# Stores on GpSimd's queue, loads on SyncE's queue, the first norm's gain applied in PSUM evictions, and dilated attention with the two heads of a pair side by side

## The chip, the cores and the metric

The kernel runs on one core of one Trainium2 chip. The metric is device time in microseconds (us) of one execution of the whole program. Engines are named as in the profile: PE is TensorE's matmuls, PEld its weight loads, DVE is VectorE, ACT is ScalarE, POOL is GpSimd, SP is SyncE. SPq and POOLq rows are the DMA issues of these two queues.

## The reference, cut to what matters

Two layers work on one sequence of 1024 tokens of width 1024, all in float32.

```
first_block:   h = rmsnorm(x, norm_gain);  proj = h @ w_in
               o_a = attention over all 1024 keys (8 query heads, 2 key heads, rotary) * silu(g_a)
               o_b = neighbourhood attention on a 16 x 64 grid (8 heads of 64)          * silu(g_b)
               x = x + [o_a, o_b] @ w_out;  x = rmsnorm(x, final_norm_gain)
second_block:  h = rmsnorm(x, norm_w);     proj = h @ w_in_2
               y_dn  = gated delta rule, 4 heads of 128, chunks of 64
               y_att = dilated attention, 8 heads of 64, patterns (window, dilation) =
                       (128, 1), (512, 4), (2048, 16), joined by their log-sum-exp, * silu(gate)
               x = x + [y_dn, y_att] @ w_out_2
```

The first norm is `x * rsqrt(mean(x*x) + eps) * norm_gain`, and the gain is one factor for each of the 1024 channels. A query of a dilated pattern sees the keys of its residue class in its own block and the block before it.

## The kernel before, in words

Tokens lie in eight tiles of 128. A product in full precision is made of three float32r matmuls: each operand is split into a rounded high part (ACT copies, `hh` or `whi`) and the rest (DVE subtracts, `hl` or `wlo`).

The **opening** (lines 549 to 575) loads the eight tiles of x (512 KB each) and the gain `ng`, repeated over 128 partitions (another 512 KB). It takes the tiles two at a time: ACT squares each tile with a row sum (line 561), DVE finds the inverse root in eleven small steps (`rs_of`, lines 286 to 297), and the tile is multiplied by the gain (line 563) and the root (lines 570 to 574). `H1.put` then transposes a tile by PE in two PSUM banks of four 128 x 128 blocks, and evicts each bank with one ACT copy (`hh`, line 315) and one DVE subtraction (`hl`, line 316), both 128 x 512. The first weights are loaded in `fill1` (line 1061) and split by lines 354 and 355.

After that two streams share the engines. `main` runs the attentions and the delta rule; `fill` runs the projections and the output products. `share` (line 465) emits them in turn by the PE time they have spent, and the Tile scheduler orders each engine's instructions by priority and by its own simulated clock. The order on an engine or a queue is then fixed.

**Queues.** `ld` and `st` are both SyncE's queue (lines 185 and 187), and so are four stores that are written with `ld` (lines 592, 603, 1350, 1364). `gl` is GpSimd's queue and has only the operands of the neighbourhood attention (`k2`, `vv` and `qT`, lines 795, 796 and 824): 44 loads. A DMA whose data or buffer isn't ready holds everything behind it on its queue. Many results go through DRAM: stored by one stage and loaded by a later one (`qa_d`, `bq_d`, `o_d`, `xp_d`, `raw_d`, `ab_d`, `tb_d`, `n_d`, `yp_d`). Stores leave from small staging buffers; the `e5` pool has four of 256 KB, which weights and residual rows are loaded into as well (line 519).

**Dilated attention** (`jobs_c`, line 1544) runs for four pairs of heads j. A pair has 24 items of 128 queries: eight of the pattern with dilation 4 (strided by 4 in q and k; half of them have one key tile, half two), eight of the pattern with dilation 16 (strided by 8, one key tile), and eight of the dense pattern (the first has one key tile, the others two). An item (line 1556) makes for each head two score matmuls (`qq` and `ql` as weights, `k2` as the moving operand, 128 or 256 columns), a masked minimum on DVE (line 1568), an exponential on ACT (1570), transposes of P on PE, a copy to `PTc` on ACT (1581), and the value matmuls (line 1588): float32, which the trace records as two passes each, with 64 columns of `v` moving, for one head. DVE copies the result to N (1592). While a pair is in work, `prep_c` prepares the next. `fill` at that time is `first_part(2, ...)` (line 909), in half-tiles of 12 matmuls of 512 columns: each loads a residual row block into an `e5` buffer (line 915), adds the product (917 or 919) and stores it (920) to `yp_d`. Its second part waits until the pairs 0 to 2 are done.

Of the kernel before, what the change touches and what calls it, by code (L numbers as in the profile page):

```python
# [32 lines left out]
NT = 8  # L33
KC = 8
# [26 lines left out]
SC = ['s']  # L61
SD = ['s']
XPR = 5000
XS = 1
LASTC = {1: 6, 2: 7}
LEAD2 = 1000.0
LEAD3 = 1000.0
# [7 lines left out]
LB = 1000.0  # L75
KO = 1
CP = 'S'
CO = 'V'
CHP = 0
AHP = 0  # L80
BHP = 0
# [72 lines left out]
def hybrid_kernel(ctx: ExitStack, tc: tile.TileContext, A, out, dbg=None, upto=99):  # L154
    nc = tc.nc
    V, S = nc.vector, nc.scalar
# [26 lines left out]

    PE = _PE()
    ld = nc.sync.dma_start
    gl = nc.gpsimd.dma_start
    st = nc.sync.dma_start
    dbg = dbg or {}

    def dram(t, off, ap):  # L190
        return bass.AP(tensor=t.tensor, offset=t.offset + off, ap=ap)
# [4 lines left out]
    sm = ctx.enter_context(tc.tile_pool(name="sm", bufs=3))  # L196
# [33 lines left out]
    def tbank():  # L230
        half[0] ^= 256
        return po_[:, half[0]:half[0] + 256]
# [13 lines left out]
    def wbank():  # L246
        return bank("w")
# [7 lines left out]
    def f32(t):  # L255
        return t.bitcast(F32)
# [13 lines left out]
    ident = f32(identr)  # L270
# [271 lines left out]
    r_d = dp.tile([8, 1024], F32, name="r_d")  # L542


    w1 = A["w_in"][0]
    H = {}
    hr.open("h1")
    H1 = Tr(hr, KC)
    with tc.tile_pool(name="xp", bufs=2, reuse_waits="tile") as xp:
        ng = xp.tile([128, 1024], F32, name="ng", bufs=1)  # L550
        for b in range(0, NT, 2):
            ss = sm.tile([128, 2], F32, name="ssx")
            xg = []
            for i in (b, b + 1):
                xt = xp.tile([128, 1024], F32, name="xt", bufs=8)
                with tc.high_priority(XPR):
                    ld(xt, grid(x_in, i))
                    if i == 0:
                        ld(ng, dram(A["norm_gain"], 0, [[0, 128], [1, 1024]]))
                scr = xp.tile([128, 1024], F32, name="sqrow", bufs=1)  # L560
                S.activation(scr, xt, AF.Square, accum_out=ss[:, i - b:i - b + 1])
                if b:
                    V.tensor_tensor(xt, xt, ng, op=OP.mult)
                xg.append(xt)
            rs = rs_of(ss, 2, 1.0 / 1024)
            for i in (b, b + 1):
                xn = xg[i - b]
                r1 = rs[:, i - b:i - b + 1]
                if b and i % 2 and XS:
                    S.activation(xn, xn, AF.Copy, scale=r1)  # L570
                elif b:
                    V.tensor_scalar(xn, xn, r1, None, op0=OP.mult)
                else:
                    V.scalar_tensor_tensor(xn, xn, r1, ng, op0=OP.mult, op1=OP.mult)
                H1.put(xn, i)

    def make_bias():
        rb = wk.tile([33, 8], F32, name="rb")
        V.memset(rb, 1.0)
        tb8 = wk.tile([8, 32], F32, name="tb8")  # L580
        ld(tb8, A["rel_bias_2"])
        tb = tbank()
        PE.transpose(tb[0:32, 0:8], tb8, ident[0:8, 0:8])
        V.tensor_copy(rb[0:32], tb[0:32, 0:8])
        oh = wk.tile([33, 1024], F32, name="oh")
        ld(oh, A["oh"])
        rr = wk.tile([8, 1024], F32, name="rr")
        for c in range(2):
            tb = sbank()
            PE.matmul(tb[0:8, :], rb, oh[:, c * 512:(c + 1) * 512], start=True, stop=True)  # L590
            V.tensor_copy(rr[:, c * 512:(c + 1) * 512], tb[0:8, :])
        ld(r_d, rr)


    wk.open("rpp")
    if 1:
        make_bias()
        rp = wk.tile([8, 32, 48], F32, name="rp")
        V.memset(rp, 0.0)
        r0 = wk.tile([8, 15, 31], F32, name="rp0")  # L600
        ld(r0, A["na_rpb"][0])
        V.tensor_scalar(rp[:, 8:23, 8:39], r0[:, ::-1, ::-1], 8.0, None, op0=OP.mult)
        ld(rp_d, rp)
    wk.close()

    def finish_pair(o2, den2, dst):
# [182 lines left out]
    def prep_b(j, B):  # L789

        yield from wait("B%d" % j)
        k2 = wm.tile([128, 2, 1024], F32R, name="k2", bufs=2)
        vv = wm.tile([128, NT, 2, 128], F32, name="vv", bufs=2).rearrange("p t h d -> p (t h d)")[:, 0:1024].rearrange("p (t c) -> p t c", t=NT)
        for a in range(2):
            gl(k2[64 * a:64 * a + 64], dram(bq_d[j], (2 + a) * 128 * 1024, [[1024, 64], [64 * 1024, 2], [1, 1024]]))
        gl(vv, bv_d[j].rearrange("(t p) c -> p t c", p=128))
        if j == 0:
            wk.close()
            wk.open("pb")
        if j == 0:  # L800
            masks.append(wk.tile([128, 3, 3, 16, 8], F32, name="masks"))
            ld(masks[0].rearrange("p v g r c -> p (v g r c)"), A["c1"][:, 1152:2304])
        tab = wk.tile([128, 2, 3, 384], F32, name="tab", bufs=2)
        B[j] = k2, vv, tab
        for h in range(2):

            tr = wk.tile([128, 16, 64], F32, name="tr")
            t3 = tr.rearrange("p r c -> p (r c)")[:, 0:768]
            ld(t3, dram(rp_d, (2 * j + h) * 32 * 48, [[48, 16], [1, 8], [1, 768]]))
            t3 = t3.rearrange("p (r c) -> p r c", c=48)[:, ::-1, ::-1]  # L810
            for v in range(3):
                V.tensor_tensor(tab[:, h, v].rearrange("p (g r c) -> p g r c", g=3, c=8),
                    t3[:, :, 24 - 8 * v:48 - 8 * v].rearrange("p r (g c) -> p g r c", c=8), masks[0][:, v], op=OP.add)
        yield 0.5

    def attn_b(j, B, live, then=None):
        k2, vv, tab = B.pop(j)
        qTs = {}

        def prep(b):  # L820

            qTs[b] = wk.tile([128, 4, 256], F32R, name="qT", bufs=QB)
            for a in range(2):
                gl(qTs[b][64 * a:64 * a + 64], dram(bq_d[j], b * 256, [[1024, 64], [64 * 1024, 4], [1, 256]]))

        def item(i, h, qT, two):

# [230 lines left out]
        yield from mark("op1")  # L1058

    def fill1():  # L1060
        ws, _ = load_w(w1, [(512, 0, 1, 256), (0, 0, 1, 256)])
# [91 lines left out]
    def delta_main():  # L1153
# [20 lines left out]
        def main2():  # L1174
# [164 lines left out]
            def chain(u):  # L1339
# [5 lines left out]
                for k in range(2):  # L1345
                    am = tc4()
                    V.tensor_tensor(am, Hs[k]["An"], bm[:, None, :].to_broadcast([128, 4, 128]), op=OP.mult)
                    ac = wk.tile([128, 4, 16], F32, name="ac", bufs=2)
                    V.tensor_reduce(ac, am.rearrange("p t (b c) -> p t c b", c=16), op=OP.add, axis=AX.X)
                    ld(dram(ab_d[u], k * 8192, [[16, 128], [2048, 4], [1, 16]]), ac)  # L1350
# [7 lines left out]
                for r in range(1, 16):  # L1358
# [5 lines left out]
                ld(tb_d[u], Tn.rearrange("p r c -> p (r c)"))  # L1364


                def join(mask, Tn_, Tt, H):
# [176 lines left out]
    def jobs_c(j):  # L1544
# [11 lines left out]
        def item(q, k, vs, T, N, then=None):  # L1556
# [2 lines left out]
            nkt = len(vs)  # L1559
            nk = 128 * nkt  # L1560
            s = sbank()
            sh = [s[:, h * nk:(h + 1) * nk] for h in range(2)]
            for h in range(2):
                PE.matmul(sh[h], qq[:, h, q], k2[:, h, k], start=True, stop=False)
                PE.matmul(sh[h], ql[:, h, q], k2[:, h, k], start=False, stop=True)
            P = wk.tile([128, 2, 256], F32, name="Pc", bufs=CB)
            for h in range(2):
                V.tensor_tensor_reduce(out=P[:, h, :nk], in0=sh[h], in1=T[:, h, T.shape[2] - nk:], op0=OP.add, op1=OP.min,  # L1568
# [16 lines left out]
            o = pbank()  # L1585
            for h in range(2):
                for t, v in enumerate(vs):
                    PE.matmul(o[:, h * 64:h * 64 + 64], PT[:, h * nkt + t], v[:, h], start=t == 0, stop=t == nkt - 1)
            if CO[alt[0] % len(CO)] == "S":
                S.activation(N[:, 0:128], o[:, 0:128], AF.Copy)  # L1590
            else:
                V.tensor_copy(N[:, 0:128], o[:, 0:128])  # L1592
            if then:
                then()
            yield 0.43 * nkt
# [127 lines left out]
```

## Time and profile before

| | us |
|---|---|
| median of 3 runs | 1762.08 |
| lowest and highest | 1745.34, 1762.79 |
| the profiled execution, in all | 1749.34 |
| its span on the core | 1747.6 |
| PE busy (share of the span) | 1560.6 (89%) |
| DVE busy | 1121.8 (64%) |
| ACT busy | 785.3 (45%) |
| POOL busy | 28.5 (2%) |
| mean granted TensorE clock, as a share of full | 0.937 |
| moved by SyncE's queue / by GpSimd's queue | 188.34 MB / 14.68 MB |

The busy share of PE is an average over stages, and its matmul records overlap, so 89% does not mean that 11% is idle everywhere. The slices of the page and the windows of the trace show which stages have idle time. A granted clock of 1.0 is 2.4 GHz, and 0.5 is 1.2 GHz.

### The profile page before, as it was taken

How to read it: one execution, taken by the hardware profiler on the slowest of the kernel's cores; microseconds unless marked ns; L12 is line 12 of the kernel's file. 1: busy time of each engine (PE TensorE's matmuls, PEld its weight loads, DVE VectorE, ACT ScalarE, POOL GpSimd, SP SyncE). 2: the span in 40 equal slices, each digit the busy share in tenths (PEclk: the TensorE clock that was granted, in tenths of full speed). 3: DMA queues.
4: the chain of work that ended last, by engine and by line, in shares of the span. 5: the costliest groups of instructions: out<-in, count | busy, mean ns of one | idle time of the engine just before them, and what ended most of it. 6: DMA issues, size and time to landing. Idle time of an engine off the chain costs nothing. (4 is left out here: it accounts for less than half of the span.)

```text
span 1747.6 us, 27569 instructions
## 1 busy us (share of the span) xinstructions
PE 1560.6 (89%) x9362; PEld 1377.5 (79%) x9362; DVE 1121.8 (64%) x3469; ACT 785.3 (45%) x2189; POOL 28.5 (2%) x48
## 2 busy tenths in 40 slices
PE   1988999999999789996799999998999489899997
PEld 1877788989898677885677788887889478788985
DVE  5679866666573554558545768676677575767646
ACT  5235445445452432544344443534524352765631
POOL 0000000000001101100000000000000000000000
PEclk8999999999999889997899999999999879876999
DMA  7011121422226998875344323314322555433476
GB/s 173 17 61 51 56 80 63 102 79 56 83 71 162 199 256 194 223 208 145 76 113 98 96 74 85 97 51 108 91 61 71 166 174 162 136 93 87 119 229 219
DMA packets 212825, 204.79 MB, mean 117 GB/s; under 512 B 27363, under 2 KB 164763, under 8 KB 212684
## 3 DMA queue, kind: packets, MB, share of 16 engines
q1 hardware_dynamic: 202252, 188.34, 38.4%
q0 software_dynamic: 10432, 14.68, 4.9%
q8 instruction: 74, 1.21, 0.3%
q14 instruction: 67, 0.55, 0.1%
HBM read 131.83 MB, written 71.13 MB: 116 GB/s over the span
## 5 line engine op out<-in xcount | busy, mean ns | idle before, releaser
L172 PE MATMUL pw<-whi,hh 128*128 128x512 f32 (+2 forms) x1032 | 359.1, 350 | 10.5 <-DVE e L524 5.4
L172 PE MATMUL pw<-wlo,hh 128*128 128x512 f32 (+2 forms) x1032 | 357.1, 346 | 0.3 <-DVE wlo L355 0.3
L172 PE MATMUL pw<-whi,hl 128*128 128x512 f32 (+2 forms) x1032 | 356.3, 345 | 0.0
L172 PEld LDWEIGHTS pw<-whi,hh 128*128 128x128 f32 x1032 | 196.9, 192 | 31.9 <-DVE e L524 6.0
L172 PEld LDWEIGHTS pw<-wlo,hh 128*128 128x128 f32 x1032 | 197.8, 192 | 19.6 <-DVE wlo L355 0.5
L172 PEld LDWEIGHTS pw<-whi,hl 128*128 128x128 f32 x1032 | 197.4, 191 | 19.9
L355 DVE TENSOR_TENSOR wlo<-e,whi 128x512 fp32r<-128x512 f32 (+3 forms) x168 | 103.6, 624 | 73.3 <-ACT whi L354 72.3
L354 ACT ACTIVATE whi<-e 128x512 fp32r<-128x512 f32 (+3 forms) x168 | 95.3, 581 | 96.9 <-DMA e<-in_w_in_dram 71.0
L172 PE MATMUL pw<-hh,whi 128*128 128x512 f32 x320 | 129.8, 405 | 7.6 <-ACT whi L354 7.5
L172 PE MATMUL pw<-hl,whi 128*128 128x512 f32 x320 | 127.2, 398 | 0.0
L172 PE MATMUL pw<-hh,wlo 128*128 128x512 f32 x320 | 123.3, 399 | 0.0
L172 PEld LDWEIGHTS po<-vc,PTc 128*128 128x128 f32 x560 | 87.9, 228 | 12.1 <-DVE N L1592 5.4
L172 PE MATMUL po<-vc,PTc 128*128 128x64 f32 x560 | 90.2, 304 | 7.3 <-DVE N L1592 4.2
L172 PE MATMUL s<-k,qT 128*128 128x512 f32 (+1 forms) x282 | 90.1, 407 | 2.7 <-ACT PT L845 1.3
L1568 DVE CUSTOM_DVE_ANT_0 Pc<-s,tab 128x128 f32<-128x128 f32 (+1 forms) x192 | 59.6, 348 | 39.5 <-PE s L172 26.4
L172 PE MATMUL po<-PT,vv 128*128 128x256 f32 x512 | 75.9, 288 | 3.9 <-DVE PT L745 3.2
L172 PEld LDWEIGHTS pw<-hh,whi 128*128 128x128 f32 x320 | 61.1, 191 | 23.2 <-ACT whi L354 11.2
L172 PEld LDWEIGHTS po<-PT,vv 128*128 128x128 f32 x512 | 68.7, 193 | 8.7 <-DVE PT L745 5.1
L745 DVE TENSOR_TENSOR PT<-s,PT 128x512 fp32r<-128x512 f32 x77 | 52.3, 685 | 32.2 <-ACT PT L744 23.1
L736 ACT ACTIVATE P<-s,nm 128x512 f32<-128x512 f32 x77 | 52.6, 686 | 44.7 <-DVE nm L733 41.9
L840 ACT ACTIVATE Pb<-Pb,m 128x384 f32<-128x384 f32 x64 | 39.1, 612 | 73.3 <-DVE m L838 70.6
L172 PEld LDWEIGHTS pw<-hl,whi 128*128 128x128 f32 x320 | 61.2, 191 | 11.4
(398 smaller groups left out, 3364.8 us busy)
## 6 DMA issues: line engine op xcount, KB each, us to landing
e<-in_w_in_dram SPq DMA_DIRECT2D x72, 256.0 KB, 3.7
bq_d<-e SPq DMA_DIRECT2D x32, 256.0 KB, 2.2
qT<-bq_d POOLq DMA_DIRECT2D x32, 256.0 KB, 7.4
e<-in_w_out_dram SPq DMA_DIRECT2D x32, 256.0 KB, 5.9
xp_d<-mx SPq DMA_DIRECT2D x32, 256.0 KB, 3.9
yp_d<-e SPq DMA_DIRECT2D x32, 256.0 KB, 3.3
e<-in_w_in_dram SPq DMA_DIRECT2D x32, 192.0 KB, 3.4
raw_d<-e SPq DMA_DIRECT2D x24, 256.0 KB, 2.0
```

What stands on the lines that cost most here:

```text
L172: self.last = f(*a, **k).ins
L354: S.activation(hi[:, :n], raw[:, :n], AF.Copy)
L355: V.tensor_tensor(lo[:, :n], raw[:, :n], f32(hi[:, :n]), op=OP.subtract)
L736: S.activation(P[:, hf * 512:(hf + 1) * 512], ss[hf], AF.Exp, bias=nm[:, 2:3], accum_out=den[:, h, hf:hf + 1])
L745: V.tensor_tensor(dl, by4(tb), f32(dh), op=OP.subtract)
L840: S.activation(P, P, AF.Exp, bias=nm, scale=-1.0, accum_out=den[:, h:h + 1])
L1568: V.tensor_tensor_reduce(out=P[:, h, :nk], in0=sh[h], in1=T[:, h, T.shape[2] - nk:], op0=OP.add, op1=OP.min, scale=-1.0, scalar=3e38, accu ...
```

## The change

1. `st` becomes GpSimd's queue, and `gl` is dropped, so that every load is on SyncE's queue. The four stores that were written with `ld` are now written with `st`. The loads of `k2` and `qT` are declared as float32 on both sides.
2. The opening loads x in two groups of four tiles and the first weights between them in program order. The gain is loaded as 8 x 128 and transposed once by PE, so that it stands as one column of 128 factors for each channel block. The tiles are only scaled by the root. The transposes of two tiles (for the last four, of four tiles) share a bank, and the evictions apply the gain: one ACT copy with a scale and one DVE operation for each channel block, 128 x 256 for the first four tiles and 128 x 512 for the last four.
3. In dilated attention an item with one key tile multiplies each head's queries with the keys of both heads (256 columns moving), and uses the half that belongs to it. The value matmul of each head has the values of both heads moving (128 columns), and the copy to N picks the two blocks that are wanted.

```diff
-    gl = nc.gpsimd.dma_start
-    st = nc.sync.dma_start
+    st = nc.gpsimd.dma_start
...
+        g8 = xp.tile([8, 128], F32, name="g8", bufs=1)
+        ld(g8, dram(A["norm_gain"], 0, [[128, 8], [1, 128]]))
...
+        def load_x(tiles):
+            for i in tiles:
                 xt = xp.tile([128, 1024], F32, name="xt", bufs=8)
                 with tc.high_priority(XPR):
                     ld(xt, grid(x_in, i))
...
+        def normed(b):
+            ss = sm.tile([128, 2], F32, name="ssx")
+            for i in (b, b + 1):
+                scr = xp.tile([128, 1024], F32, name="sqrow", bufs=2)
+                S.activation(scr, xts[i], AF.Square, accum_out=ss[:, i - b:i - b + 1])
             rs = rs_of(ss, 2, 1.0 / 1024)
+            V.tensor_scalar(xts[b], xts[b], rs[:, 0:1], None, op0=OP.mult)
+            if b < 4:
+                V.tensor_scalar(xts[b + 1], xts[b + 1], rs[:, 1:2], None, op0=OP.mult)
+            else:
+                S.activation(xts[b + 1], xts[b + 1], AF.Copy, scale=rs[:, 1:2])
+        def flip_x(tiles, gT):
+            n = len(tiles)
+            h, l = H1.half(tiles[0] // 4)
+            c = slice(tiles[0] % 4 * 128, (tiles[0] % 4 + n) * 128)
+            m = 4 // n
+            for k0 in range(0, KC, m):
+                tb = wbank()
+                for k in range(m):
+                    for j, i in enumerate(tiles):
+                        PE.transpose(tb[:, (k * n + j) * 128:(k * n + j + 1) * 128], xts[i][:, (k0 + k) * 128:(k0 + k + 1) * 128], ident)
+                for k in range(m):
+                    t, g = tb[:, k * n * 128:(k + 1) * n * 128], gT[:, k0 + k:k0 + k + 1]
+                    S.activation(h[:, k0 + k, c], t, AF.Copy, scale=g)
+                    V.scalar_tensor_tensor(l[:, k0 + k, c], t, g, f32(h[:, k0 + k, c]), op0=OP.mult, op1=OP.subtract)
+        load_x(range(4))
...
+        for b in (0, 2):
+            normed(b)
+            flip_x((b, b + 1), gT)
+            if b == 0:
+                ws0 += load_w(w1, [(512, 0, 1, 256), (0, 0, 1, 256)])[0]
+                load_x(range(4, 8))
+        for b in (4, 6):
+            normed(b)
+        flip_x((4, 5, 6, 7), gT)
...
-            gl(k2[64 * a:64 * a + 64], dram(bq_d[j], ...))
-        gl(vv, bv_d[j].rearrange("(t p) c -> p t c", p=128))
+            ld(f32(k2[64 * a:64 * a + 64]), dram(bq_d[j].bitcast(F32), ...))
+        ld(vv, bv_d[j].rearrange("(t p) c -> p t c", p=128))
...
-            sh = [s[:, h * nk:(h + 1) * nk] for h in range(2)]
+            sh = [s[:, h * 256:(h + 1) * 256] for h in range(2)]
             for h in range(2):
-                PE.matmul(sh[h], qq[:, h, q], k2[:, h, k], start=True, stop=False)
-                PE.matmul(sh[h], ql[:, h, q], k2[:, h, k], start=False, stop=True)
+                kk = k2[:, h, k] if nkt == 2 else k2[:, :, k]
+                PE.matmul(sh[h], qq[:, h, q], kk, start=True, stop=False)
+                PE.matmul(sh[h], ql[:, h, q], kk, start=False, stop=True)
+            if nkt == 1:
+                sh = [s[:, h * 384:h * 384 + 128] for h in range(2)]
...
-                    PE.matmul(o[:, h * 64:h * 64 + 64], PT[:, h * nkt + t], v[:, h], start=t == 0, stop=t == nkt - 1)
+                    PE.matmul(o[:, h * 128:h * 128 + 128], PT[:, h * nkt + t], v.rearrange("p h d -> p (h d)"),
+                              start=t == 0, stop=t == nkt - 1)
...
-                V.tensor_copy(N[:, 0:128], o[:, 0:128])
+            V.tensor_copy(N[:, 0:128].rearrange("p (h d) -> p h d", h=2), o.rearrange("p (a d) -> p a d", d=64)[:, 0::3])
```

## Rows read from the trace of the kernel before

**Rows 1.** The page, part 2: the granted clock in 40 slices, in tenths of full speed.

```profile
PEclk8999999999999889997899999999999879876999
```

**Rows 2.** Windows: stretch, length, then busy PE, PEld, DVE, ACT, POOL, clock, DMA, GB/s.

```profile
1000.00:1200.00 200.00, 196.59 (x1144) 171.43 (x1142) 141.10 (x397) 87.11 (x247) 0.00 (x0) 0.99 0.34 83
1380.00:1404.00 24.00, 0.14 (x1) 0.17 (x2) 9.89 (x43) 6.96 (x22) 0.00 (x0) 0.54 0.65 192
1490.00:1660.00 170.00, 155.71 (x915) 146.25 (x916) 117.95 (x509) 111.61 (x390) 0.00 (x0) 0.81 0.38 109
1539.00:1559.00 20.00, 19.47 (x94) 19.13 (x94) 9.97 (x52) 10.20 (x42) 0.00 (x0) 0.50 0.37 107
```

**Rows 3.** Timeline of the opening: start, length, instruction, [idle before and its end].

```profile
3.39 0.51 SPq L559 DMA_DIRECT2D ng<-in_norm_gain_dram  x1
...
13.65 1.06 ACT L561 ACTIVATE sqrow<-xt 128x1024 f32<-128x1024 f32 x1 [3.23 <-DMA xt<-in_x_dram]
...
15.88 1.06 ACT L561 ACTIVATE sqrow<-xt 128x1024 f32<-128x1024 f32 x1 [1.08 <-DMA xt<-in_x_dram]
...
24.87 2.48 DVE L574 SCALAR_TENSOR_TENSOR xt<-xt,rq_y,ng 128x1024 f32<-128x1024 f32 x2
...
26.30 1.08 PE L172 MATMUL s<-ident,xt 128*128 128x128 f32 x4 [26.30 <-DVE xt L574]
...
49.28 0.39 PE L172 MATMUL pw<-whi,hh 128*128 128x256 f32 x1 [0.53 <-DVE rb L579]
```

**Rows 4.** Groups of DVE instructions in the first 50 us: total, mean ns, idle before.

```profile
L563 DVE TENSOR_TENSOR xt<-xt,ng 128x1024 f32<-128x1024 f32 x6 | 7.3, 1224 | 3.1 <-ACT sqrow L561 3.0
...
L316 DVE TENSOR_TENSOR hl<-s,hh 128x512 fp32r<-128x512 f32 x8 | 5.4, 682 | 1.3 <-ACT hh L315 1.3
...
L572 DVE TENSOR_SCALAR xt<-xt,rq_y 128x1024 f32<-128x1024 f32 x3 | 2.2, 748 | 0.0
L289 DVE TENSOR_TENSOR rq_a<-rq_y 128x2 f32<-128x2 f32 x12 | 1.7, 154 | 0.1
```

**Rows 5.** Timeline where the delta rule ends: SyncE's issues around a store, and PE's next matmul.

```profile
1373.51 0.42 SPq L889 DMA_DIRECT2D e<-g_d  x1
...
1384.22 2.29 SPq L1452 DMA_DIRECT2D o_d<-orr  x2
...
1386.56 0.98 SPq L1487 DMA_DIRECT2D trc<-r_d  x2
...
1403.86 1.08 PE L172 MATMUL pw<-ident,e 128*128 128x128 f32 x4 [23.89 <-DVE rq_ac L290]
```

**Rows 6.** Timeline of PE: float32 matmuls of the delta rule, dilated scores, value matmuls.

```profile
1060.33 1.06 PE L172 MATMUL s<-Tt,da 128*128 128x128 f32 x8
...
1377.32 1.29 PE L172 MATMUL s<-da,da 128*128 128x256 f32 x4
1378.80 1.16 PE L172 MATMUL s<-da,da 128*128 128x128 f32 x4
...
1464.94 1.19 PE L172 MATMUL s<-da,da 128*128 128x128 f32 x4
...
1704.18 1.00 PE L172 MATMUL po<-vc,PTc 128*128 128x64 f32 x8
```

**Rows 7.** DMA issues (KB each, median us to landing), then landing times of GpSimd's qT loads.

```profile
yp_d<-e SPq DMA_DIRECT2D x32, 256.0 KB, 3.3
...
e<-yp_d SPq DMA_DIRECT2D x16, 256.0 KB, 4.1
...
DMA to landing us min/median/max: 3.7/7.4/11.9
```

**Rows 8.** Waits of the queues: total us, times, longest.

```profile
SPq L915 <- DMA yp_d<-e: 51.4, 23, 5.0
...
POOL qT L824 <- PE s L172: 121.2, 10, 24.1
```

**Rows 9.** The chain of waits: start, length, piece, with the count of its instructions.

```profile
1669.36 4.12 PE pw L172 x18
```

More of the change, by code (lines that the diff above doesn't have):

```diff
@@ L63 @@
 XPR = 5000
-XS = 1
 LASTC = {1: 6, 2: 7}
@@ L77 @@
 CP = 'S'
-CO = 'V'
 CHP = 0
@@ L548, in hybrid_kernel @@
     H1 = Tr(hr, KC)
+    ws0 = []
     with tc.tile_pool(name="xp", bufs=2, reuse_waits="tile") as xp:
[L550 to L554, printed above, removed]
+        g8 = xp.tile([8, 128], F32, name="g8", bufs=1)
+        ld(g8, dram(A["norm_gain"], 0, [[128, 8], [1, 128]]))
+        xts = []
+        def load_x(tiles):
+            for i in tiles:
                 xt = xp.tile([128, 1024], F32, name="xt", bufs=8)
@@ L557, in hybrid_kernel @@
                     ld(xt, grid(x_in, i))
[L558 to L564, printed above, removed]
-            rs = rs_of(ss, 2, 1.0 / 1024)
[L566 to L575, printed above, removed]
+                xts.append(xt)
@@ new lines, in hybrid_kernel @@
+        load_x(range(4))
+        tb = tbank()
+        PE.transpose(tb[:, 0:8], g8, ident[0:8, 0:8])
+        gT = xp.tile([128, 8], F32, name="gT", bufs=1)
+        V.tensor_copy(gT, tb[:, 0:8])
+        for b in (0, 2):
[7 more added lines that the diff above has]
+        flip_x((4, 5, 6, 7), gT)
@@ L591, in make_bias @@
             V.tensor_copy(rr[:, c * 512:(c + 1) * 512], tb[0:8, :])
-        ld(r_d, rr)
+        st(r_d, rr)
     wk.open("rpp")
@@ L602, in hybrid_kernel @@
         V.tensor_scalar(rp[:, 8:23, 8:39], r0[:, ::-1, ::-1], 8.0, None, op0=OP.mult)
-        ld(rp_d, rp)
+        st(rp_d, rp)
     wk.close()
@@ L794, in prep_b @@
         for a in range(2):
-            gl(k2[64 * a:64 * a + 64], dram(bq_d[j], (2 + a) * 128 * 1024, [[1024, 64], [64 * 1024, 2], [1, 1024]]))
-        gl(vv, bv_d[j].rearrange("(t p) c -> p t c", p=128))
+            ld(f32(k2[64 * a:64 * a + 64]), dram(bq_d[j].bitcast(F32), (2 + a) * 128 * 1024, [[1024, 64], [64 * 1024, 2], [1, 1024]]))
+        ld(vv, bv_d[j].rearrange("(t p) c -> p t c", p=128))
         if j == 0:
@@ L823, in prep @@
             for a in range(2):
-                gl(qTs[b][64 * a:64 * a + 64], dram(bq_d[j], b * 256, [[1024, 64], [64 * 1024, 4], [1, 256]]))
+                ld(f32(qTs[b][64 * a:64 * a + 64]), dram(bq_d[j].bitcast(F32), b * 256, [[1024, 64], [64 * 1024, 4], [1, 256]]))
         def item(i, h, qT, two):
@@ L1060, in fill1 @@
     def fill1():
-        ws, _ = load_w(w1, [(512, 0, 1, 256), (0, 0, 1, 256)])
+        ws = ws0
         yield from proj_kv(ws, rt, kv)
@@ L1349, in chain @@
                     V.tensor_reduce(ac, am.rearrange("p t (b c) -> p t c b", c=16), op=OP.add, axis=AX.X)
-                    ld(dram(ab_d[u], k * 8192, [[16, 128], [2048, 4], [1, 16]]), ac)
+                    st(dram(ab_d[u], k * 8192, [[16, 128], [2048, 4], [1, 16]]), ac)
                 Ab = wk.tile([64, 16, 16], F32, name="Ab")
@@ L1363, in chain @@
                     yield Y1
-                ld(tb_d[u], Tn.rearrange("p r c -> p (r c)"))
+                st(tb_d[u], Tn.rearrange("p r c -> p (r c)"))
                 def join(mask, Tn_, Tt, H):
@@ L1587, in item @@
                 for t, v in enumerate(vs):
-                    PE.matmul(o[:, h * 64:h * 64 + 64], PT[:, h * nkt + t], v[:, h], start=t == 0, stop=t == nkt - 1)
-            if CO[alt[0] % len(CO)] == "S":
-                S.activation(N[:, 0:128], o[:, 0:128], AF.Copy)
-            else:
-                V.tensor_copy(N[:, 0:128], o[:, 0:128])
+                    PE.matmul(o[:, h * 128:h * 128 + 128], PT[:, h * nkt + t], v.rearrange("p h d -> p (h d)"),
+                              start=t == 0, stop=t == nkt - 1)
+            V.tensor_copy(N[:, 0:128].rearrange("p (h d) -> p h d", h=2), o.rearrange("p (a d) -> p a d", d=64)[:, 0::3])
             if then:
```

## The prediction

> **What bounds the kernel now.** I read the page first: PE is busy 89% of the span (the table), and the granted clock falls in some slices only [rows 1]. So I looked for the stages where PE idles or runs at the lower clock, with the windows and the waits of PE. From 1000 to 1200 us PE is busy 196.6 of 200 us [rows 2]: there a cheaper store or load buys nothing, and only matmuls count. Three stages are different, and the change touches each.
>
> First, the opening. PE's first transposes start at 26.3 us and the first projection matmul at 49.28 us [rows 3]. Everything behind them follows in order, so time won here moves the whole rest forward.
>
> Second, the end of the delta rule, where PE does nothing for 23.9 us up to 1403.86 [rows 5]; the window shows 0.14 us of PE in 24 [rows 2]. SyncE's queue shows why: after a load at 1373.51 it issues nothing until the store of `orr` at 1384.22, which waits for DVE, and the bias tables that the first dilated items need (`trc`) stand behind it, at 1386.56 [rows 5].
>
> Third, dilated attention without `fill`, 1490 to 1660: the mean clock is 0.81 [rows 2], so at two levels some 65 us (170 x 0.19 x 2) run at 1.2 GHz. One such stretch, 1539 to 1559, has PE busy 19.47 of 20 us at 0.50 [rows 2], while it did strided one-key-tile items with 64-column value matmuls.
>
> **The opening: -12 us.** The gain's 512 KB stand in the queue between the first and the second x tile (issued at 3.39); tiles land 2.2 us apart (squares of tiles 1 and 2 wait for DMA until 13.65 and 15.88) [rows 3]. Without it tile 1 is squared at about 11.4. Then the root: eleven small steps of 0.154 us [rows 4], issued some 0.2 us apart when nothing comes between. Before, they end only at 24.87 [rows 3], some ten us after the second square, because gain multiplications of 1.224 us stand between them in DVE's order [rows 4]. After: 11.4 + 1.25 for the square and its sum + 2.2 + two scalings of 0.748 [rows 4] = 16.4, against 26.3. The end of the stage gains less, since DVE becomes the limit: six scalings (4.5 us), eight evictions of 0.682 (5.5), sixteen of half the width (between 0.34 and 0.682, I take 0.4, near the halving: 6.4), eight weight subtractions like the 0.682 ones (5.5) and 44 small steps (6.8) are 29 us from about 12, hence 41. But the first half of H1 is complete well before, so projections of tiles 0 to 3 can fill PE from about 35. I take the first projection matmul at 37 in place of 49.3. Bounds: -4 (the scheduler puts all transposes and evictions first and the scale in the eviction costs DVE more) and -20 (the projection of four tiles is done before the last tile is evicted).
>
> **Stores off the load queue: -8 us.** In the hole the table loads can go as soon as their buffers are free, up to 10.7 us (1384.22 - 1373.51) earlier [rows 5]. What is late next is `fill`: its next rows of `o2_d` come from that very store, which will now land later, so only a part of the 23.9 us goes. I take -8, with 0 (the table buffers lie where the last delta tiles are) and -24 (the whole hole) as ends. The 470 stores or so, counted from the loops, cost GpSimd time that nothing else wants. The 44 loads that come to SyncE's queue were waiting for buffers on a queue of their own: `qT` waited 121.2 us in ten waits, the longest 24.1 [rows 8]. Where the planned order errs, such a wait now holds the loads of `fill`. I take 0, because the planner places the load where it expects the buffer free; ends 0 and +10.
>
> **Slower landing of stores: +5 us.** A store on GpSimd's queue isn't in this trace. The nearest rows are its 256 KB loads: 3.7 us at least, 7.4 in the median, against 3.3 for the `yp_d` store on SyncE's [rows 7]. So a round trip through DRAM grows by 0.4 to 4.1 us in most cases. Most of them (`qa_d`, `bq_d`, `raw_d`, `c_d`) are loaded much later. Those of the delta chain (eight trips, up to 33 us together) lie under `fill` while PE is busy 98% [rows 2]; without that cover they would cost it. On the path stand the last output store (+3) and some buffers (+2). Ends 0 and +12.
>
> **Wider matmuls: 0 us.** Eight value passes of 64 columns take 1.00 us, and eight float32 passes of 128 columns 1.06 [rows 6]; over 560 passes 4 us at most, part of it beside other work. For the scores, four 256-column matmuls strided by 4 take 1.29 us and four 128-column ones 1.16 [rows 6]: width is nearly free there. Strided by 8, 128 columns take 1.19 [rows 6], and 256 columns aren't shown: between 1.19 and twice that, or +38 us for 32 items at the far end. I take the near end, since the stride of 4 is nearest.
>
> **Clock: -6 us.** The same items now move twice the columns in value matmuls and one-key-tile scores. If the 65 us at 1.2 GHz rose to 2.4, half of them at most would go (-32). But strided scores take the same time at both widths, and ACT and DVE are busy two thirds of that window [rows 2], so I put the whole at -18 and take a third of that, because no row says that the clock will rise. Ends 0 and -32.
>
> **Sum:** -12 - 8 + 5 + 0 - 6 = -21 us. Against the profiled execution, 1749.3, that is 1728. That execution lies 12.7 us under the median of the runs (1762.1), which lie at 1745 and at 1762 to 1763; I add half of that distance and predict **1734 us**.
>
> **Rivals.**
> A. *Only the opening gains.* SyncE's row says that the store held the tables; the wait may be for their buffers in any case. The Trainium skill, "DMA: Bandwidth & Descriptors", section "Issuing engines are not separate DMA queues", says that starting DMAs from several engines saves only the sequencer's time to initiate them. By that rule the 23.9 us hole stays; the 10.7 us in which the queue issued nothing speak against it. With hole 0, clock 0 and stores +5 the sum is -7: 1742 from the profiled execution, 1748 by the same half step.
> B. *Slower: staging buffers.* A half-tile of `first_part(2)` holds one of four `e5` buffers through load (4.1 us), add (0.7) and store (3.3) [rows 7]: 8.1 us, or 2.0 a half-tile, below PE's 12 x 0.23 = 2.8 (18 such matmuls take 4.12 us [rows 9]). SyncE already waits 51.4 us in 23 waits for such stores [rows 8]. With 7.4 us to land it is 12.2, or 3.05; with 11.9 [rows 7] it is 16.7, or 4.2, and PE would wait 1.4 us for each of 32 half-tiles: +45. It decides from 11.2 us a cycle on, a landing of 6.4. Against it: a store no longer waits on its queue behind the next load. Price: -21 + 45 = +24, so 1773, or 1779 by the half step.
> C. *All of it.* The hole closes to a few us (-18), the clock stays up (-18), opening -16, stores +5: -47, hence 1702, or 1708.
>
> **Numbers.** Forecast 0.49, A 0.26, B 0.16, C 0.09. One per cent, about what a measurement of this kernel can tell, is 17.6 us. The forecast and C are faster (0.58), A is within it (with its upper tail and that of the forecast, 0.26), B slower (0.16). The forecast's own range, from the bounds of opening and hole, is 1715 to 1750; with C's centre and two thirds of B's cases the range is 1706 to 1770.
>
> **What would show it.** Right: first transposes near 16 us and the first projection matmul before 40; the hole at the end of the delta rule under 18 us with `trc` issued before the `orr` store is ready; eight value passes still near 1.0 us; clock near 1.0 in the strided items of the second and third pairs; POOL with some 500 issues. Wrong: `yp_d` landing over 6.4 us with PE waiting behind line 917 or 919; four stride-8 scores well over 1.3 us; SyncE waiting long on `qT` or `k2`.

## The result, and the profile after

The changed kernel took 1705.5 us (median of four runs, 1703.5 to 1706.1) against 1755.7 for the kernel before on the same chip: a ratio of 0.972, 95% interval 0.966 to 0.978. The profiled execution took 1705.8 us (span 1704.1). The prediction of 1734 was too slow, and its range began at 1706. One run of `e1_queues` (2174.8 us) and one of `e4_gain_first` (1738.4 us) were slow, at a lower granted clock (0.647 and 0.876), and are left out below, so that their medians are 1707.6 and 1701.5 where expectations written earlier say 1710 and 1702.

The page, part 2 and 3, of the changed kernel: the granted clock in 40 slices, the packets, and its two large queues (packets, MB, share of the 16 engines).

```profile
PEclk7999999999999899998899999999999979999999
...
DMA packets 163675, 204.28 MB, mean 120 GB/s; under 512 B 22395, under 2 KB 118331, under 8 KB 163532
...
q1 hardware_dynamic: 138476, 131.35, 28.5%
q0 software_dynamic: 25056, 71.16, 12.3%
```

Against [rows 1] the slices of dilated attention, the 35th to 37th, no longer fall to 0.8, 0.7 and 0.6; what is left is the hole before it. The stores are now on the software queue. The windows of the changed kernel (stretch, length, busy PE, PEld, DVE, ACT, POOL, clock, DMA share, GB/s) answer to [rows 2]: first a stretch of dilated attention, then neighbourhood attention whole.

```profile
1464.00:1632.00 168.00, 156.21 (x987) 144.67 (x986) 119.67 (x512) 111.90 (x397) 21.15 (x33) 0.98 0.40 123
...
558.00:761.00 203.00, 182.56 (x1099) 161.52 (x1099) 110.54 (x335) 90.35 (x238) 34.56 (x65) 0.93 0.82 232
```

The same neighbourhood stage of the kernel before, of which the prediction quotes no row:

```profile
567.00:786.00 219.00, 189.77 (x1113) 168.31 (x1112) 112.42 (x335) 91.83 (x239) 21.47 (x34) 0.90 0.90 216
```

It is 16 us shorter, with PE idle for 20 us in place of 29 and the clock at 0.93 in place of 0.90. Dilated attention with the tail after it became 16 us shorter too (327 from 343 us, from the first transpose of `Pc` to the end), the delta rule 7, the first attention 4, the opening 6; the stretch between the neighbourhood stage and the delta rule is 5 longer. The timeline of the opening after, to set against [rows 3]:

```profile
14.57 0.45 PE L170 MATMUL s<-ident,xt 128*128 128x128 f32 x1 [14.57 <-DVE xt L567]
...
23.17 0.27 PE L170 MATMUL po<-ident,g 8*128 8x8 f32 x1 [5.15 <-DMA g<-in_norm_gain_dram]
...
31.05 1.08 PE L170 MATMUL s<-ident,xt 128*128 128x128 f32 x4 [6.57 <-DVE hl L587]
...
40.61 1.73 PE L170 MATMUL pw<-ident,xt 128*128 128x128 f32 x8
43.65 0.39 PE L170 MATMUL pw<-whi,hh 128*128 128x256 f32 x1 [1.31 <-DVE hl L587]
```

The first transposes start at 14.6 in place of 26.3, but the first projection matmul only at 43.7 in place of 49.3. In PE's order it stands behind the last transposes, at 40.61. The end of the delta rule, to set against [rows 5]:

```profile
1350.74 1.14 SPq L1514 DMA_DIRECT2D trc<-r_d  x2
...
1360.47 0.76 POOL L1479 DMA_DIRECT2D o_d<-orr  x1 [24.54 <-DVE rq_yd L288]
...
1368.07 0.33 SPq L913 DMA_DIRECT2D e<-o_d  x1
...
1375.13 0.68 DVE L917 TENSOR_TENSOR e<-e,e 128x512 f32<-128x512 f32 x1
...
1375.96 1.09 PE L170 MATMUL pw<-ident,e 128*128 128x128 f32 x4 [19.53 <-DVE rq_ac L287]
```

The first tables (`trc`) do go out before the store, and it helps little: PE's next matmul in its order needs the rows that this store writes and that are loaded again at 1368.07. PE idles 19.5 us here and some 22 in all between the stages, against 23.9. The transfers after (KB each, median us to landing) answer to [rows 7]:

```profile
qT<-bq_d SPq DMA_DIRECT2D x32, 256.0 KB, 7.5
...
xp_d<-mx POOLq DMA_DIRECT2D x32, 256.0 KB, 4.4
yp_d<-e POOLq DMA_DIRECT2D x32, 256.0 KB, 3.2
```

A store lands as fast from GpSimd's queue as it did from SyncE's (3.2 and 3.3 us for `yp_d`), and `qT` takes as long in the two kernels (7.5 and 7.4 us).

### The profile page after: what moved, and what is told of

The parts are those of the page before. It is cut to its first block, busy times and chain, and to the rows that moved or that the text cites. A ratio compares the mean times of both kernels' runs of the same rounds, so it can differ in the third digit from the quotient of the medians.

```text
span 1704.1 us, 27867 instructions
## 1 busy us (share of the span) xinstructions
PE 1537.7 (90%) x9363; PEld 1354.6 (79%) x9363; DVE 1119.9 (66%) x3473; ACT 782.9 (46%) x2196; POOL 261.3 (15%) x474
## 2 busy tenths in 40 slices
DMA packets 163675, 204.28 MB, mean 120 GB/s; under 512 B 22395, under 2 KB 118331, under 8 KB 163532
## 5 line engine op out<-in xcount | busy, mean ns | idle before, releaser
L170 PE MATMUL po<-vc,PTc 128*128 128x128 f32 x560 | 83.3, 284 | 8.7 <-DVE N L1622 7.0
L170 PEld LDWEIGHTS po<-vc,PTc 128*128 128x128 f32 x560 | 75.4, 197 | 13.7 <-DVE N L1622 6.7
L1601 ACT ACTIVATE Pc<-Pc,Nst 128x128 f32<-128x128 f32 (+1 forms) x128 | 53.6, 422 | 36.7 <-DVE Nst L1599 34.4
L170 PEld LDWEIGHTS pw<-hh,wlo 128*128 128x128 f32 x320 | 60.2, 189 | 11.7
```

The source lines that it names most:

```text
L170: self.last = f(*a, **k).ins
L1601: S.activation(P[:, h, :nk], P[:, h, :nk], AF.Exp, bias=N[:, 128 + h:129 + h], scale=-1.0, accum_out=N[:, 130 + h:131 + h])
```

## The experiments

Times are medians, ratios are to the kernel before run beside each kernel (1752 to 1757 us), with 95% intervals in brackets.

**One part alone.** `e1_queues` has only the queue lines of the change, `e2_opening` only the opening, `e3_dilated` only the dilated attention.

```diff
# e1_queues (and the other stores and loads named in the change)
-    gl = nc.gpsimd.dma_start
-    st = nc.sync.dma_start
+    st = nc.gpsimd.dma_start
# e2_opening
-            for i in (b, b + 1):
-                xn = xg[i - b]
...
+            normed(b)
+            flip_x((b, b + 1), gT)
# e3_dilated
-                    PE.matmul(o[:, h * 64:h * 64 + 64], PT[:, h * nkt + t], v[:, h], start=t == 0, stop=t == nkt - 1)
+                    PE.matmul(o[:, h * 128:h * 128 + 128], PT[:, h * nkt + t], v.rearrange("p h d -> p (h d)"),
...
+                kk = k2[:, h, k] if nkt == 2 else k2[:, :, k]
```

> The kernel before with the new queues alone (stores on GpSimd's, loads on SyncE's), opening and dilated attention as before. Against 1755.7 of the kernel before. Theory 1 (the queues gave the 16 us of the neighbourhood stage, by fewer packets and no load waiting behind a store): 1735 to 1741, the stage from 550 to 790 us shorter by 10 or more, the DMA packets near 164,000, the hole before the dilated items still about 20 us or more. Theory 2 (the queues only save the time of issuing; the stage was shorter by its order of work and the clock that came with it): 1750 to 1758. My prediction's terms for this part (-8 and +5) would give 1753.

Measured: 1707.6, ratio 0.974 (0.969 to 0.979). The queues alone give 45 of the 50 us, more than either theory said. Of the 42 us in the profiled executions, 21 lie in the neighbourhood stage (561 to 759 us), 11 from the first transpose of `Pc` to the end (332 from 343), and 6 ahead of the neighbourhood stage. PE's hole before dilated attention is 20.2 us.

> The kernel before with the new opening alone (gain as an 8x128 load, applied in the evictions). Theory 1 (the gain's small load stands behind eight x tiles and holds the first evictions): first transposes near 15 us, first projection matmul near 44, and 1750 (-6). My prediction's term gave -12: 1744. Theory 2 (the opening's gain is lost or multiplied further back by another order of work): outside 1745 to 1753 with the first projection still near 44.

Measured: 1744.0, ratio 0.994 (0.992 to 0.997): 8 us less than the kernel before beside it. The interval is 6 to 15 us, so it does not tell theory 1's 6 from the prediction's 12. The first transposes start at 14.7 and the first projection at 44.1; what holds the latter is tested with `e4_gain_first` below.

> The kernel before with the new dilated attention alone (both heads side by side in the value matmuls and in the one-key-tile scores). Theory 1 (wider matmuls keep the granted clock up): the stretch of the dilated items without other work at a mean clock near 0.97 in place of 0.81, and 1734 to 1740 (-16 to -20). Theory 2 (the clock stayed up in the changed kernel because the queues or the order of the work changed): the clock there 0.80 to 0.88, and 1752 to 1758. My prediction's term gave -6: 1750.

Measured: 1745.3, ratio 0.995 (0.993 to 0.998): 7 us less, with 3 to 13 in the interval. The clock from 1490 to 1660 is 0.98, so theory 1 is right on the clock and wrong on the time: a clock that rises by a fifth gave, with the wider matmuls that raise it, 7 us, near the prediction's 6, and not 18.

**Order or queue.** The order of each engine's instructions is planned when the program is built, and a change of queues is also a change of order: in `e1_queues` 5,258 of PE's 8,438 instructions stand at another place than before. Two kernels part them. In both, instructions of PE, DVE and ACT are chained by scheduling edges without semaphores, in an order taken from another kernel:

```diff
+    force_order(tc)
...
+            inst = tc.nc.find_inst_by_name("I-" + n)
...
+                tc.add_manual_dep(inst, prev, mybir.DependencyInfo(
+                    mybir.DependencyClass.NoSync, mybir.DependencyReason.SCHED_ONLY), reason="given order")
```

`g1_newq_oldorder` is `e1_queues` held in the order of the kernel before, `g2_oldq_neworder` the kernel before held in the order of `e1_queues`. The order of the DMAs on a queue is not held: of the 510 loads other than k2, vv and qT, 461 stand at the same place in `g2_oldq_neworder` as in `e1_queues`.

> The new queues alone (as in e1_queues, 1710 against 1752), but with every instruction of TensorE, VectorE and ScalarE held in the order of the kernel before, so that only the queues differ. Theory 1 (the chip's queues gave the 42 us: transfers start or land sooner): 1705 to 1720. Theory 2 (the planner, which sees the other queues, found a better order, and the queues themselves give little): 1742 to 1758.

> The mirror image: the queues of the kernel before, with TensorE's, VectorE's and ScalarE's instructions held in the order of e1_queues. Theory 1 (the queues themselves gave it): 1745 or more, slower than before if the order asks for data that the old queue brings late. Theory 2 (the order gave it): 1705 to 1720.

Measured: 1735.3 (ratio 0.989, 0.983 to 0.994) and 1740.2 (0.991, 0.987 to 0.995). Neither theory stands alone. By the ratios the queues in the old order are worth some 20 us, the new order on the old queues some 16, and both together 46. Each of these is known to some 8 us, so the totals could be a plain sum. In the neighbourhood stage, with one profiled execution each, they need each other: 217 and 218 us with one, 219 with none, 198 with both. Is the order's part only a lucky draw? Two kernels change one number of the planner:

```diff
-R1 = 1.0
+R1 = 1.01
```

> The kernel before with one number of its planner changed (R1, the ratio of main work to fill work in the two attention stages, 1.0 to 1.01): another order, the same work and queues. It asks how far any new order moves the time. Theory 1 (an order is only as good as the queues that it is made for): 1747 to 1761 against 1753. Theory 2 (the order of before was a poor draw, and most others are 10 us or more better): 1728 to 1743.

> The new queues alone with the same change of the planner's number (R1 1.0 to 1.01). Theory 1 (with the new queues the planner finds good orders as a rule): 1702 to 1718. Theory 2 (the order of e1_queues was a lucky draw): 1722 to 1740.

Measured: 1751.8 (ratio 1.000, 0.998 to 1.003) and 1708.5 (0.975, 0.971 to 0.979). Another order that the planner makes for the old queues (2,466 of 9,362 matmuls at another place) moves nothing, though the order of `e1_queues`, held on them, gave 16 us. The new queues' gain stays under another order. One other order each does not show how all orders behave, but neither time looks like a draw.

**What the queue does.** With the same order, `g2_oldq_neworder` and `e1_queues` can be laid side by side matmul by matmul (9,362 in each, in the same sequence). The former falls behind by 8 us up to 595 us, by another 4 to 675, and by 6 at one matmul that needs rows of `o_d` loaded again; some 14 more are lost from 1370 us on, in the hole and in dilated attention. The timeline of `g2_oldq_neworder` there:

```profile
732.32 0.48 DVE L885 SCALAR_TENSOR_TENSOR oa<-po,rd,gb 128x64 f32<-128x64 f32 x2 [0.33 <-PE po L194]
...
737.28 0.32 SPq L937 DMA_DIRECT2D mx<-xp_d  x1
737.70 0.38 SPq L942 DMA_DIRECT2D xp_d<-mx  x1
738.13 0.42 SPq L1034 DMA_DIRECT2D vv<-xp_d  x1
738.65 0.40 SPq L942 DMA_DIRECT2D xp_d<-mx  x1
739.10 0.45 SPq L887 DMA_DIRECT2D o_d<-oa  x1
...
745.38 0.37 SPq L908 DMA_DIRECT2D e<-o_d  x1
...
750.43 0.69 PE L194 MATMUL p<-ident,e 128*128 128x128 f32 x2 [7.85 <-DMA e<-o_d]
```

And that of `e1_queues` at the same instructions:

```profile
719.74 0.48 DVE L862 SCALAR_TENSOR_TENSOR oa<-po,rd,gb 128x64 f32<-128x64 f32 x2 [0.33 <-PE po L172]
...
720.51 0.54 POOL L864 DMA_DIRECT2D o_d<-oa  x1 [1.50 <-DVE rd L857]
...
726.33 0.37 SPq L885 DMA_DIRECT2D e<-o_d  x1
...
732.12 0.69 PE L172 MATMUL p<-ident,e 128*128 128x128 f32 x2 [2.11 <-DMA e<-o_d]
```

With one queue the result `oa`, ready at 732.8, is stored at 739.1, because a load that has to wait (`mx`, at 737.28) stands ahead of the store; with two it goes out after 0.3 us. The load of it follows 6 us after the store in both, so PE waits 7.85 in place of 2.11 us. This is one place of many: it shows the mechanism for 6 of the 31 us between the two profiled executions. Two more theories were open: that the moved loads do it, or that the transfers load the DMA engines less. `f1_stores_only` moves the stores and leaves k2, vv and qT on GpSimd's queue; `g4_loads_back` is that in the order of `e1_queues`; `g3_two_stores` moves two kinds of stores only; `g5_all_on_sp` puts all on SyncE's queue.

```diff
# f1_stores_only and g4_loads_back, against e1_queues (k2, vv and qT by gl again)
+    gl = nc.gpsimd.dma_start
# g3_two_stores, against g2_oldq_neworder
-                    st(o_d[r], od)
+                    nc.gpsimd.dma_start(o_d[r], od)
-                st(dst[r], xt)
+                nc.gpsimd.dma_start(dst[r], xt)
# g5_all_on_sp, against e1_queues with its order held
-    st = nc.gpsimd.dma_start
+    st = nc.sync.dma_start
```

> The stores on GpSimd's queue, with the loads of k2, vv and qT left there too, as they were before; SyncE keeps the other loads. Theory 1 (taking the stores off SyncE's queue is what counts): 1705 to 1718, like e1_queues. Theory 3 (the moved loads count: a load that waits for its buffer on GpSimd's queue would now hold the stores behind it): 1725 to 1765.

> The order of e1_queues held, all stores on GpSimd's queue, but the loads of k2, vv and qT left on GpSimd's queue too, as in f1_stores_only (1729, which had an order of its own). Theory 1 (a load that waits for its buffer there holds the stores behind it, so the loads have to leave the stores' queue): 1722 to 1735. Theory 2 (the 18 us between f1_stores_only and e1_queues come from the order): 1707 to 1716.

> The queues of the kernel before and the order of e1_queues held, as in g2_oldq_neworder (1740), but with two kinds of stores on GpSimd's queue: those of the residual rows (xp_d and yp_d, 64 stores of 256 KB) and those of the neighbourhood's output (o_d from oa, 64 stores of 64 KB). They are about 20 MB of some 63 MB stored. Theory 1 (a result waits on SyncE's queue behind a load that waits, and these stores are on the way from one result to the next): most of the 30 us between g2_oldq_neworder and e1_queues (1710), so 1712 to 1722. Theory 3 (all transfers run better because the stores take fewer packets on GpSimd's queue): a third of it, 1727 to 1733.

> The order of e1_queues held and every load and store on SyncE's queue: the fourth corner beside e1_queues (two queues, 1710), g4_loads_back (stores and the loads of k2, vv, qT on GpSimd's, 1721) and g2_oldq_neworder (only those loads on GpSimd's, 1740). Theory 1 (what counts is that nothing waits behind another's wait in one queue): 1745 or more, since all now stand in one row. Theory 3 (the transfers of k2, vv and qT load the DMA engines less from SyncE's queue: 166 us busy in the neighbourhood stage of e1_queues, 186 in g4_loads_back): less busy DMA engines than g2_oldq_neworder (194 us in that stage) and 1720 to 1736.

Measured: `f1_stores_only` 1728.6 (0.986, 0.980 to 0.993), `g4_loads_back` 1721.1 (0.981, 0.977 to 0.985), `g3_two_stores` 1724.4 (0.982, 0.977 to 0.986), `g5_all_on_sp` 1741.5 (0.995, 0.993 to 0.997). The four corners with the order of `e1_queues` held are then: all on SyncE's queue 1741.5; only the moved loads on GpSimd's 1740.2; stores and moved loads on GpSimd's 1721.1; only the stores there 1707.6. So the stores are worth 19 or 34 us, by where the loads are, and moving the loads nothing with the stores on SyncE's queue and 13 with them on GpSimd's (21 with the order free). The edit that moves k2 and qT also declares them float32, and no run parts the two. `g4_loads_back` came out just under theory 1's range, `f1_stores_only` in theory 3's. `g3_two_stores` moved 90 stores (26 of them of `oa`, where the expectation counted 64) and gave half of the 33 us, between its two theories, and little in the neighbourhood stage (216 of 218 us). GpSimd's queue and DVE there:

```profile
625.81 0.57 POOL L887 DMA_DIRECT2D o_d<-oa  x1 [12.46 <-DVE oa L885]
626.37 1.25 POOL L846 DMA_DIRECT2D qT<-bq_d  x2
```

```profile
625.04 0.47 DVE L885 SCALAR_TENSOR_TENSOR oa<-po,rd,gb 128x64 f32<-128x64 f32 x2 [8.30 <-DMA gb<-g_d]
```

Now a load (`qT`) stands behind a store that waits 12.5 us for its result: the same pattern on the other queue. But PE waits for `qT` only 2.6 us in this whole stage, and the result itself had waited 8.3 us for the gate rows `gb`, loaded by SyncE's queue 18 us earlier, in a stretch (600 to 625 us) where the DMA share is 1.24. So late landing has a part here, and why `g3_two_stores` gains little in this stage is not shown. `g5_all_on_sp` asks whether waiting or the load on the DMA engines counts. The neighbourhood stage of it, then of `g2_oldq_neworder`, then of `e1_queues` (columns as above):

```profile
559.00:777.00 218.00, 188.86 (x1104) 166.84 (x1102) 111.39 (x336) 90.85 (x238) 0.00 (x0) 0.90 0.79 218
```

```profile
560.00:778.00 218.00, 189.98 (x1105) 166.45 (x1104) 111.38 (x336) 90.62 (x239) 21.41 (x34) 0.89 0.88 216
```

```profile
561.00:759.00 198.00, 181.70 (x1099) 161.03 (x1098) 110.46 (x334) 89.99 (x238) 35.01 (x65) 0.94 0.84 238
```

With everything on SyncE's queue the DMA engines are busy 0.79 of the stage in place of 0.88, and the stage is as long. With two queues they are busy 0.84, and it is 20 us shorter. So less load on the DMA engines does not by itself shorten the stage. That a DMA which waits holds its row fits all four corners and is seen at the matmul above; that the relief gained something which the longer row took again is not excluded. `g5_all_on_sp`, with runs from 1734.9 to 1747.4, lies about theory 1's bound and above theory 3's range.

**The opening.** `e4_gain_first` loads the gain ahead of x.

```diff
-        ld(g8, dram(A["norm_gain"], 0, [[128, 8], [1, 128]]))
+        with tc.high_priority(XPR + 1):
+            ld(g8, dram(A["norm_gain"], 0, [[128, 8], [1, 128]]))
```

> The changed kernel with the gain's 4 KB load ahead of the x tiles. Theory 1 (it stood behind them, landed at 23 us and held the first evictions from 18 us on): first evictions near 17, first projection matmul at 35 to 39, and 1696 to 1701 against 1705.5. Theory 2 (the evictions' time on DVE and ACT sets the end of the opening): first evictions earlier but the first projection still at 42 to 44, 1704 to 1707.

Measured: 1701.5, ratio 0.970 (0.966 to 0.973), between the two theories' ranges and not told apart from the changed kernel. The timeline, and the window from 21 to 45 us:

```profile
4.73 0.24 PE L170 MATMUL po<-ident,g 8*128 8x8 f32 x1 [4.73 <-DMA g<-in_norm_gain_dram]
...
45.32 0.58 PE L170 MATMUL pw<-whi,hh 128*128 128x256 f32 x1 [0.86 <-DVE hl L588]
```

```profile
21.00:45.00 24.00, 12.73 (x48) 8.71 (x48) 20.23 (x61) 18.41 (x37) 0.00 (x0) 1.00 0.41 112
```

The gain lands 18 us earlier and the first projection still starts at 45, released by one of the last evictions of DVE, which is busy 20.2 of 24 us. Theory 2 holds on the mechanism: the late gain cost next to nothing, and DVE's list of scalings, evictions and weight casts sets the end, with PE's order, in which the projections come last. An order with projections between the evictions was not run.

**Dilated attention.** `h1_narrow_scores` and `h2_narrow_values` undo one widening each in the changed kernel; `e5_opening_queues` is `e4_gain_first` without the edit of `e3_dilated`, with neither widening.

```diff
# h1_narrow_scores (and its halves of s as before)
-                kk = k2[:, h, k] if nkt == 2 else k2[:, :, k]
+                kk = k2[:, h, k]
# h2_narrow_values (and its copy to N as before)
-                    PE.matmul(o[:, h * 128:h * 128 + 128], PT[:, h * nkt + t], v.rearrange("p h d -> p (h d)"),
+                    PE.matmul(o[:, h * 64:h * 64 + 64], PT[:, h * nkt + t], v[:, h], start=t == 0, stop=t == nkt - 1)
```

> The changed kernel with the one-key-tile scores narrow again (128 columns of one head), value matmuls still 128 columns wide. Theory 1 (the wide value matmuls keep the clock up): at most 15 us at the lower clock in the dilated stage, as in the changed kernel, and 1700 to 1709. Theory 2 (the wide scores are needed for it): 30 to 75 us at the lower clock there, and 1706 to 1720.

> The changed kernel with the value matmuls 64 columns wide again (one head), one-key-tile scores still wide. Theory 1 (the wide value matmuls keep the clock up, but twice the columns at the full clock take as long as half the columns at the lower one): 50 us or more at the lower clock in the dilated stage, and 1702 to 1711. Theory 2 (the scores keep it up): at most 25 us there, and 1695 to 1704, since the value matmuls are then shorter.

> The changed kernel with the gain's load ahead of the x tiles and dilated attention as before: the new queues and the new opening without the wider matmuls. Theory 1 (on top of the new queues the wider matmuls buy nothing): 1698 to 1705, like e4_gain_first (1702). Theory 2 (they are worth the 7 us of e3_dilated here too): 1706 to 1714.

Measured: 1710.0 (ratio 0.973, 0.968 to 0.979), 1700.7 (0.970, 0.966 to 0.974), 1700.8 (0.971, 0.967 to 0.974). In the dilated stage PE was busy at the lower clock for 73 us in `e1_queues`, 13 in the changed kernel, 19 in `h1_narrow_scores`, 18 in `h2_narrow_values` and 56 in `e5_opening_queues`. So either widening alone does most of it: for `h2_narrow_values` theory 2 came out, in clock and time, and `h1_narrow_scores` lies between its two. But neither kernel is clearly faster or slower than the changed one, and without both widenings (`e5_opening_queues`, 1700.8) the time is that with both (`e4_gain_first`, 1701.5). From the first transpose of `Pc` to the end the profiled executions took 328 and 330 us. So theory 1 of `e5_opening_queues` holds: on top of the queues they buy nothing that these runs can tell. The window of `e1_queues` at narrow width:

```profile
1464.00:1632.00 168.00, 159.17 (x957) 151.49 (x958) 118.09 (x518) 113.14 (x406) 18.72 (x28) 0.81 0.38 111
```

At 0.98 the changed kernel got 987 matmuls into the same 168 us, at 0.81 this one 957: a clock higher by a fifth, 3% more matmuls. The mix is not quite the same: the former have wider scores, and 45 projection matmuls of 512 columns where the latter have 6. The value matmuls of these windows, by shape (total us, mean ns), in `e1_queues`, the changed kernel and `h2_narrow_values`:

```profile
L172 PE MATMUL po<-vc,PTc 128*128 128x64 f32 x404 | 66.8, 312 | 1.1 <-DVE N L1591 1.0
```

```profile
L170 PE MATMUL po<-vc,PTc 128*128 128x128 f32 x398 | 59.2, 285 | 5.0 <-DVE N L1622 3.6 <-DVE Nst L1622 1.3
```

```profile
L170 PE MATMUL po<-vc,PTc 128*128 128x64 f32 x399 | 54.5, 272 | 1.6 <-DVE N L1620 1.3
```

Between the two kernels with narrow values the mean goes from 312 to 272 ns at the higher clock, and the width gives 13 back.

**A version of both.** `k1_best` is `h2_narrow_values` with the edit of `e4_gain_first`.

> The changed kernel with the gain's load ahead of the x tiles and the value matmuls 64 columns wide again (scores wide): the two experiments that came out below the changed kernel, together. If both gains are real and add: 1695 to 1699. If VectorE sets the end of the opening in any case: 1699 to 1703, like h2_narrow_values. If the two only came from another order: 1703 to 1708.

Measured: 1703.5, ratio 0.971 (0.968 to 0.974), in its third range: the two do not add, and of all these versions none is shown to be faster than the changed kernel.

## Why the prediction was wrong

**Stores off the load queue: the step that failed.** It priced the queues at -8, at one place, the hole of [rows 5]. The queues gave 45 us (`e1_queues`), and the hole 4 of them (20.2 us for 23.9). Rival A was right on the outcome, but not by its reason, the tables' buffers. By the trace the prediction's own reason was the right one (the next rows of `o2_d` come from that very store), only for most of the 23.9 us and not for a part. Most of the gain lies elsewhere: 21 us in the neighbourhood stage, of which the prediction quoted no row and where stores of results and loads that wait for buffers stood in one row, and 11 in dilated attention with the tail, where it had priced only clock and width. None of its windows [rows 2] covers the neighbourhood stage, where PE is idle 29 of 219 us. The one row of SyncE's waits that it took, 51.4 us for `yp_d` stores [rows 8], was used for rival B and is not where the gain came from: that wait is longer in the changed kernel. Rows of the other kind, a store that waits for its result with every load behind it, were there in the kernel before. The waits of SyncE's queue, before and then after:

```profile
SPq L865 <- DVE oa L863: 16.4, 9, 10.1
```

```profile
SPq L942 <- DMA yp_d<-e: 64.5, 21, 6.9
```

**The moved loads: 0.** With the stores on SyncE's queue that is what the runs show (1740.2 and 1741.5). With the stores on GpSimd's queue, where the change puts them, it is -13 (order held). The wait of 121.2 us on GpSimd's queue [rows 8] was read as harmless. Whether the 13 us are those of stores held behind such waits was not traced.

**The planner's order** was no term at all. By the ratios it is worth some 16 us on the old queues and 26 on the new, of 46. The planner made it with the new queues; the other order that it made for the old ones (`j1_replan_before`) gave nothing.

**Slower landing: +5, measured about 0.** `yp_d` lands in 3.2 us for 3.3, `xp_d` in 4.4 for 3.9; from PE's last matmul to the end of the kernel it is 4.9 us for 3.9. The nearest row had been GpSimd's loads of `qT` at 7.4 us [rows 7]; they take 7.5 from SyncE's queue in the changed kernel, so that row told of the load and not of how fast a store lands from GpSimd's queue. With it rival B falls.

**The opening: -12, measured -8** (`e2_opening`), and 6 in the trace. The first transposes came as said. What failed is the sentence that projections of tiles 0 to 3 would fill PE from 35: PE's order puts them behind the transposes of the last tiles, as the prediction's own bound of -4 had it, and these wait for DVE, so they start at 44. DVE's own sum in the prediction said 41; its half-width evictions took 0.47 us where it had 0.4.

**Clock and width: -6 and 0, measured -7 alone** (`e3_dilated`) **and nothing that shows on top of the queues.** The sum is right by luck, from two errors. The clock did rise all the way, from 0.81 to 0.98, which the prediction had put at -18 whole; it gave far less. And width was not free, as single groups in [rows 6] had suggested: 285 against 272 ns is 7 us over 560 value matmuls (busy time), and the same stretch held only 3% more matmuls at the higher clock.

**The range** reached down to 1706, just past rival C's centre (1708). The forecast's own range has a slip: with opening -20 and hole -24 its lower end is 1710 and not 1715. C's total came true, by other places than C named: hole -18 did not happen, and the queues' part elsewhere made up for it; that was luck. The Trainium skill, "DMA: Bandwidth & Descriptors", section "Issuing engines are not separate DMA queues", says that more issuing engines save only the sequencer's time to initiate a DMA. Taken as a bound on the gain, the runs disagree: with the order held, one queue for all took 1741.5 us and two 1707.6. At the matmul traced above it was a wait in the row that cost the time, and not the 0.3 to 0.5 us of an issue.

**Open:** the 8 us that the one-queue kernels lose at the start of the neighbourhood stage, where the DMA engines are busiest, and the 14 from 1370 us on were not traced to single instructions as the 6 us were; late landing may have a part in them. How much of the 13 us of the moved loads comes from their declaration as float32 is open too; and what else paces the dilated stage at the full clock, beyond the 7 us of the value matmuls, was not measured by itself.

## What to carry to other kernels

Before pricing a change of queues, list for every stage what waits in a queue's row and what stands behind it, loads behind stores and stores behind loads; the price is the sum over all stages and not the one place where a stall is plain. Where a scheduler plans the order with a model of the queues, run the new queues in the old order and the old queues in the new order, since the gain can need both. A clock that rises is no gain by itself: look whether the same number of matmuls then takes less time.

## What the runs showed of the hardware that was not expected

Some 204 MB in both took 163,675 packets in place of 212,825, and in the neighbourhood stage the DMA engines' busy share fell from 0.90 to 0.82, with no time to show for that by itself (0.79 in `g5_all_on_sp` and 0.88 in `g2_oldq_neworder`, with stages of 218 us). GpSimd's queue, with 0.54 to 0.76 us for an issue, landed 256 KB stores within 0.5 us of SyncE's. The `qT` loads, 7.4 and 7.5 us to land from GpSimd's and SyncE's queue in the kernels before and after, took 4.4 with everything on SyncE's queue (`g5_all_on_sp`). And 128-column value matmuls took 285 ns at a clock of 0.98 where 64-column ones took 312 at 0.81 and 272 at 0.97.
